# Attention in a hybrid encoder: four buffers of probabilities instead of two, and three constants of the recurrences moved into the recurrences' own pools

## The chip, the cores and the metric

The kernel runs on one core of a Trainium2 chip. The metric is the device time of one execution in microseconds (us). The core's engines work side by side, each through its own list of instructions in order: PE is TensorE's matmuls, PEld its weight loads, DVE is VectorE, ACT is ScalarE, POOL is GpSimd, SP issues most of the DMAs.

## The reference

Two layers over a sequence of 1024 tokens of width 1024. Layer 0 projects the input once and feeds two groups of heads: eight heads of windowed softmax attention with three dilations and one shared bias (A), and four heads of a gated recurrence in both directions (B). Layer 1 has twelve heads of another gated recurrence (C). Each ends in a gate, an output projection and a LayerNorm.

```
x = inputs                                          # 1 x 1024 x 1024, float32
for layer in (0, 1):
    if layer == 0:
        proj = x @ w_in_ab
        oa = dilated_attention(qa, ka, va, rel_bias)   # per pattern (1, 4, 16): s = q.k/8 + bias, |offset| <= 64 steps
                                                       # p = softmax(s); o = p.v; merged over patterns by denominators
        ob = rmsnorm(fwd_scan(q, k, v, g_f) + bwd_scan(q, k, v, g_b) - diag)
        y = (concat(oa, ob) * silu(gate)) @ w_out_ab
    else:
        y = (rmsnorm(bidirectional_scan(silu(q), 1 - f, log f, i)) * silu(gate)) @ w_out_c
    x = layer_norm(sqrt(2) * x + y) * gain + bias
```

## The kernel before, in words

All products in float32 are made of parts: each operand is split into a high part rounded to fp32r (a cast on ScalarE) and the rest (a subtraction on VectorE), and three matmuls high x high, low x high, high x low are added up in PSUM. `project` (L225 to L227) does this for the input projections: 128 output rows by 512 tokens take 8 x 3 matmuls of 512 columns. `out_units` (L247 to L249) does it for the output projections, each group of three followed by an addition to z on VectorE (L252).

The three dilated patterns of the attention are one softmax here: the bias of a key carries the logarithm of how many patterns hold it. Heads are taken in four pairs (`AttnPair`). One call of `qtile` handles 128 queries of one head: score matmuls (L571, L572) into two banks of PSUM with the tag `s`, which has two buffers; VectorE adds the bias strip in three passes and takes the running maximum (L583, 512, 64 and 128 wide), writing a tile `p` of 128 x 704; ScalarE takes the exponential and its sum; VectorE takes the reciprocal (L587) and multiplies (L588). `pv` takes two such tiles: twelve transposes on TensorE (L599) into the PSUM tiles `tr` and `kv`, high parts pH on ScalarE (L604) and low parts pL on VectorE (L605), products with the values (L608, L609, L616, L618), and a merge of the two halves of the output (L625, L626). A pair has 16 calls of `qtile` and 8 of `pv`, 32 of `pv` in all.

The low parts of the keys lie in eight tiles `kl`, whose unused half is zeroed once (`low_tile`, L461).

Constants in use: `ident` for transposes; `restart`, a row of zeros and ones that restarts the running sum of the recurrences every 16 steps (scan, L711); `mask`, for the scores of the forward direction; `ones`, which sums squares over partitions for the norm. The last three are used by layers' recurrences alone. All lie in the pool `const`, which lives through the kernel. The attention's tiles lie in a pool of their own, as do those of the GLA heads and of the HGRN heads; one is closed before the next is opened, and the tiles of the new one lie where the old one's were.

What sets the order: the program names its work as units (a projection of one block, a `qtile`, a `pv`, ...), merges the units of each head pair or head by hand-set places (`WIN`, `LAST`), and hands them to a scheduler. This gives each engine a fixed list: an instruction can be placed when its operands and a free buffer for its output are there by the scheduler's own estimate. With two buffers of `p`, the scores' passes of a third query tile are placed behind the transposes of the first. At run time each engine takes its list in order and waits for semaphores.

GpSimd's DMAs (`strip`, restored tiles `E` and `F`, gate weights `upr`) are written as descriptors into a region of SBUF whose size is `dynamic_dma_scratch_size`.

Of the kernel before, what the change touches and what calls it, by code (L numbers as in the profile page):

```python
# [7 lines left out]
F32 = mybir.dt.float32  # L8
F32R = mybir.dt.float32r
U32 = mybir.dt.uint32  # L10
# [5 lines left out]
P = 128  # L16
# [4 lines left out]
HALF = 512  # L21
# [8 lines left out]
BUCKETS, MAX_DIST = 32, 1024  # L30
# [13 lines left out]
RUN = 512  # L44
# [393 lines left out]
class AttnPair(Item):  # L438
# [92 lines left out]
    def core(self):  # L531
        T, nc, pool = self.T, self.T.nc, self.pool
        units = []
        st = {}

        def strip(j):

            t = pool.tile([P, SW], F32, tag="strip", name="strip", bufs=2)
            row = self.line[2 * self.hp + j:2 * self.hp + j + 1, :]
            st["strip", j] = t  # L540

            def src(off, step, n, w):
                return bass.AP(tensor=row.tensor, offset=row.offset + off, ap=[[1, P], [step, n], [1, w]])

            nc.gpsimd.dma_start(t[:, 0:SB].rearrange("p (b c) -> p b c", c=P), src(128, RUN, 7, P))
            nc.gpsimd.dma_start(t[:, SB:SC].rearrange("p (b c) -> p b c", c=P), src(3 * RUN, 256, 2, P))
            for h in range(2):
                tc_ = t[:, SC + 112 * h:SC + 112 * h + 112].rearrange("p (b c) -> p b c", c=16)
                for b0, n in ((0, 3), (4, 3)):
                    nc.gpsimd.dma_start(tc_[:, b0:b0 + n, :], src(b0 * RUN + 112 + 144 * h, RUN, n, 16))  # L550
                nc.gpsimd.memset(tc_[:, 3, :], -1e30)

        def qtile(j, h, r):
            if j == 0 and h == 0 and r == 0:
                self.held = {}
                self.yH = [pool.tile([P, HALF], F32R, tag="yH", name="yH", bufs=2) for _ in range(2)]
                self.yL = [pool.tile([P, HALF], F32R, tag="yL", name="yL", bufs=2) for _ in range(2)]
            if h == 0 and r == 0:
                strip(j)
            p = st[r % 2] = pool.tile([P, 704], F32, tag="p", name="p", bufs=2)  # L560
            m = pool.tile([P, 6], F32, tag="m", name="m", bufs=4)
            qi = self.q[j][h][:, r, :]
            sp = []
            for g in (h, 1 - h):
                s_ = T.ps.tile([P, HALF], F32, tag="s", name="s", bufs=2)
                if g == h:
                    out, keys = s_, lambda t: t[:, 64:KW]
                else:
                    out = s_[:, 0:2 * P].rearrange("p (b c) -> p b c", c=P)
                    keys = lambda t: bass.AP(tensor=t.tensor, offset=t.offset, ap=[t.ap[0], [64 + P * r, 2], [1, P]])  # L570
                nc.tensor.matmul(out, qi, keys(self.kh[j][g]), start=True, stop=False)  # L571
                nc.tensor.matmul(out, qi, keys(self.kl[j][g]), start=False, stop=True)  # L572
                sp.append(s_)
            t = st["strip", j]

            def rev(lo, n):
                return t[:, lo:lo + n][:, ::-1]

            parts = [(p[:, 0:512], sp[0], rev(P * r, 512)),
                     (p[:, 512:576], sp[1][:, 0:64], rev(SC + 112 * h + 16 * r, 64)),  # L580
                     (p[:, 576:704], sp[1][:, P:2 * P], rev(SB + P * h, P))]
            for n, (o, a, b) in enumerate(parts):
                nc.vector.tensor_tensor_reduce(o, a, b, 1.0, -3.0e38 if n == 0 else m[:, n - 1:n],  # L583
                                               op0=ALU.add, op1=ALU.max, accum_out=m[:, n:n + 1])
            nc.vector.tensor_scalar(m[:, 3:4], m[:, 2:3], -1.0, None, op0=ALU.mult)
            T.act(p, p, AF.Exp, bias=m[:, 3:4], accum_out=m[:, 4:5])
            nc.vector.reciprocal(m[:, 5:6], m[:, 4:5])  # L587
            nc.vector.tensor_scalar(p, p, m[:, 5:6], None, op0=ALU.mult)  # L588
# [71 lines left out]
class ScanHead(Item):  # L660
# [109 lines left out]
    def keys(self, d, hf):  # L770

        T, nc, pool, V = self.T, self.T.nc, self.pool, self.V
        r = self.pr[d, hf]
        tiles = [t for t in range(4) if hf * 4 + t != (NT - 1 if d == 0 else 0)]
        tp = T.ps.tile([P, 4, P], F32, tag="tr", name="tr", bufs=1)
        for t in tiles:
            nc.tensor.transpose(tp[:, t, :], r["k3"][:, t * P:(t + 1) * P], T.ident)  # L777
        k3T = pool.tile([P, 4, P], F32, tag="k3T", name="k3T", bufs=self.nbuf)
        lo, hi = tiles[0], tiles[-1] + 1
        nc.scalar.copy(k3T[:, lo:hi, :], tp[:, lo:hi, :])  # L780
        per = HALF // V
        order = tiles if d == 0 else tiles[::-1]
        for a in range(0, len(order), per):
            kv = T.ps.tile([P, per, V], F32, tag="kv", name="kv", bufs=1)
            for j, t in enumerate(order[a:a + per]):
                nc.tensor.matmul(kv[:, j, :], k3T[:, t, :], self.v[:, hf * 4 + t, :], start=True, stop=True)  # L786
            for j, t in enumerate(order[a:a + per]):
                i = hf * 4 + t
                nx = i + 1 if d == 0 else i - 1
                if d == 0:  # L790
                    self.stf[nx] = pool.tile([P, V], F32, tag="stf", name="stf", bufs=4)
                    dst, old = self.stf[nx], self.stf.get(i)
                else:
                    dst, old = self.stb[:, nx, :], self.stb[:, min(i, NT - 2), :]
                if i == (0 if d == 0 else NT - 1):
                    nc.vector.tensor_copy(dst, kv[:, j, :])
                else:
                    nc.vector.scalar_tensor_tensor(dst, old, r["dec"][:, t, :], kv[:, j, :],  # L798
                                                   op0=ALU.mult, op1=ALU.add)
# [296 lines left out]
def trunk_kernel(tc, x, w_in_ab, gla_gate_up, gla_gate_bias, gla_norm, w_out_ab, w_in_c, hgrn_lower_bounds,  # L1096
                 hgrn_norm, w_out_c, rel_bias, ln_gain, ln_bias, onehot, ident, mask, out):
    nc = tc.nc
    with ExitStack() as ctx:
        T = Trunk(ctx, tc)  # L1100
        c = T.const

        def load(name, shape, src, dtype=F32, eng=None):
            t = c.tile(shape, dtype, tag=name, name=name)
            (eng or nc.scalar).dma_start(t, src)
            return t

        T.ident = load("ident", [P, P], ident)
        T.mask = load("mask", [P, P], mask, U32)
        small_consts = c.tile([P, 4], F32, tag="sc", name="sc")  # L1110
        T.eps, T.epsz, T.one = (small_consts[:, i:i + 1] for i in range(3))
        for t, val in ((T.eps, EPS), (T.epsz, EPS / ALPHA ** 2), (T.one, 1.0)):
            nc.gpsimd.memset(t, val)
        T.restart = c.tile([P, HALF], mybir.dt.uint8, tag="restart", name="restart")
        nc.gpsimd.memset(T.restart, 1)
        nc.gpsimd.memset(T.restart.rearrange("p (n c) -> p n c", c=16)[:, :, 0:1], 0)
        T.ones = c.tile([P, P], F32R, tag="ones", name="ones")
        nc.scalar.copy(T.ones, T.one.broadcast_to([P, P]))
        line = T.dram.tile([A_HEADS, NLINE], F32, name="line")

        def const(name, *shape):
# [34 lines left out]
        gp, ap, hp = Phase(tc, "gla"), Phase(tc, "attn"), Phase(tc, "hgrn")  # L1156
        lr = []

        def bias_line(q):

            sl = slice(q * RUN, (q + 1) * RUN)
            oh = ap.tile([2 * BUCKETS + 2, RUN], F32, tag="p", name="oh", bufs=2)
            nc.sync.dma_start(oh, onehot[:, sl])
            ohr = ap.tile([2 * BUCKETS + 2, RUN], F32R, tag="pH", name="ohr", bufs=2)
            with tc.issue_after(T.lastact):
                nc.scalar.copy(ohr, oh)
            ps = T.ps.tile([P, HALF], F32, tag="s", name="s", bufs=2)
            with tc.issue_after(T.lastmm):
                nc.tensor.matmul(ps[0:A_HEADS], rb, ohr, start=True, stop=True)
            ls = ap.tile([A_HEADS, RUN], F32, tag="pL", name="ls", bufs=2)  # L1170
            nc.vector.tensor_copy(ls, ps[0:A_HEADS])
            nc.scalar.dma_start(line[:, sl], ls)
# [3 lines left out]
        G = [GlaHead(T, gp, h, w_in_ab[0], w_out_ab[0], gla_gate_up[0], lr, gbias, gnorm) for h in range(B_HEADS)]  # L1176
        low = {}
        A = [AttnPair(T, ap, i, w_in_ab[0], w_out_ab[0], line, low) for i in range(A_HEADS // 2)]
        H = []
# [73 lines left out]
        units = [ap.open] + tiles(start, 0, 4)  # L1253
# [3 lines left out]
        for i in range(len(A)):  # L1257
            more = G[0].spill(ap, "kh", 6, [(n, hf) for n in range(1, PARK) for hf in range(2)]) if i + 1 == len(A) else ()
            units += step(A, i, spill=more)
        units += [ap.close, gp.open] + G[0].restore() + G[0].early()  # L1260
        for i in range(len(G)):
            units += step(G, i, ln0, H[0].spill(gp, "E", 7, [(n, 0) for n in range(5)]) if i + 1 == len(G) else ())
        units += [gp.close, hp.open] + H[0].restore() + H[0].early()
        for i in range(len(H)):
            units += step(H, i, ln1)
        units += [hp.close]
# [51 lines left out]
```

## Time and profile before

| | |
|---|---|
| median of 3 runs | 2022.54 us (2022.08 to 2022.85) |
| the profiled execution | 2024.63 us, span 2022.8 us |
| PE | busy 1936.5 us, 96 % of the span, 13151 instructions |
| PEld | 1534.1 us, 76 % |
| DVE | 1302.6 us, 64 % |
| ACT | 1012.6 us, 50 % |
| POOL | 326.4 us, 16 % |
| granted clock of TensorE, mean | 0.988 |

Busy time counts the time from an instruction's start to its end, and matmuls overlap. In the views below, the share of clock is 1.00 for TensorE's upper level. "Idle before" is the time that an engine stood before an instruction, with the instruction that released it.

### The profile page before, as it was taken

How to read it: one execution, taken by the hardware profiler on the slowest of the kernel's cores; microseconds unless marked ns; L12 is line 12 of the kernel's file. 1: busy time of each engine (PE TensorE's matmuls, PEld its weight loads, DVE VectorE, ACT ScalarE, POOL GpSimd, SP SyncE). 2: the span in 40 equal slices, each digit the busy share in tenths (PEclk: the TensorE clock that was granted, in tenths of full speed). 3: DMA queues.
4: the chain of work that ended last, by engine and by line, in shares of the span. 5: the costliest groups of instructions: out<-in, count | busy, mean ns of one | idle time of the engine just before them, and what ended most of it. 6: DMA issues, size and time to landing. Idle time of an engine off the chain costs nothing.

```text
span 2022.8 us, 33771 instructions
## 1 busy us (share of the span) xinstructions
PE 1936.5 (96%) x13151; PEld 1534.1 (76%) x13151; DVE 1302.6 (64%) x2727; ACT 1012.6 (50%) x1860; POOL 326.4 (16%) x846
## 2 busy tenths in 40 slices
PE   8999999899999999988899999999999999999997
PEld 6767777777787878866678788778778877787875
DVE  4587777775676566577674746565674565666568
ACT  4555555553544444444465545445544553554463
POOL 1111010100111011012221212111211111221124
PEclk9999999999999999999999999999999999999999
DMA  5311021211211112111311111121111111111112
GB/s 144 77 33 47 20 54 27 49 53 61 63 37 48 48 38 68 47 48 44 103 53 42 48 48 32 43 63 33 38 59 41 38 43 58 32 44 53 37 53 83
DMA packets 141274, 103.73 MB, mean 51 GB/s; under 512 B 14517, under 2 KB 122933, under 8 KB 141115
## 3 DMA queue, kind: packets, MB, share of 16 engines
q1 hardware_dynamic: 129355, 89.44, 15.0%
q0 software_dynamic: 3968, 9.77, 2.1%
q10 hardware_dynamic: 7792, 2.37, 0.5%
q8 instruction: 103, 1.69, 0.3%
q14 instruction: 56, 0.46, 0.1%
HBM read 93.71 MB, written 7.85 MB: 50 GB/s over the span
## 4 chain that ended last, share of the span: by engine, by line
PE 46%; DVE 6%; ACT 5%; issue 2%; DMA 1%; POOL 1%; DVEq 0%; ACTq 0%; POOLq 0%
PE pj L225 10%; PE pj L226 10%; PE pj L227 10%; PE kv L786 3%; DVE g L711 2%; PE po L247 2%; PE po L248 2%; PE po L249 2%; PE s L812 2%; PE o L856 1%; PE o L858 1%; PE o L860 1%; DMA wraw<-in_w_out_c_dram 1%; PE tr L700 1%; PE tr L777 1%
## 5 line engine op out<-in xcount | busy, mean ns | idle before, releaser
L225 PE MATMUL pj<-xH,wH 128*128 128x512 f32 x1600 | 639.0, 399 | 1.4 <-ACT wH L187 0.9
L226 PE MATMUL pj<-xL,wH 128*128 128x512 f32 x1600 | 636.2, 398 | 0.0
L227 PE MATMUL pj<-xH,wL 128*128 128x512 f32 x1600 | 634.8, 397 | 0.0
L225 PEld LDWEIGHTS pj<-xH,wH 128*128 128x128 f32 x1600 | 302.5, 189 | 60.9 <-ACT wH L187 1.3
L227 PEld LDWEIGHTS pj<-xH,wL 128*128 128x128 f32 x1600 | 301.7, 189 | 56.4
L226 PEld LDWEIGHTS pj<-xL,wH 128*128 128x128 f32 x1600 | 302.3, 189 | 54.5
L188 DVE TENSOR_TENSOR wL<-wraw,wH 128x512 fp32r<-128x512 f32 x210 | 147.7, 703 | 183.0 <-ACT wH L187 162.0
L187 ACT CAST wH<-wraw 128x512 fp32r<-128x512 f32 x210 | 130.0, 619 | 199.4 <-PE pj L226 169.4
L731 POOL TENSOR_TENSOR eT<-gE 128x16 f32<-128x16 f32 x64 | 31.7, 495 | 1061.7 <-ACT gE L146 1061.7
L252 DVE TENSOR_TENSOR z<-z,po 128x512 f32<-128x512 f32 x200 | 136.1, 683 | 76.1 <-PE po L249 74.4
L247 PE MATMUL po<-woH,yH 128*128 128x512 f32 x336 | 138.0, 414 | 4.1 <-ACT yH L635 2.7
L248 PE MATMUL po<-woL,yH 128*128 128x512 f32 x336 | 134.2, 399 | 1.4 <-DVE woL L206 1.4
L249 PE MATMUL po<-woH,yL 128*128 128x512 f32 x336 | 131.6, 394 | 0.0
L205 ACT CAST woH<-wraw 128x512 fp32r<-128x512 f32 x80 | 47.5, 617 | 99.3 <-PE po L249 45.7
L786 PE MATMUL kv<-v,k3T 128*128 128x128 f32 (+1 forms) x448 | 80.3, 313 | 10.5 <-DVE stb L798 4.8
L247 PEld LDWEIGHTS po<-woH,yH 128*128 128x128 f32 x336 | 62.9, 189 | 32.3 <-DVE z L252 9.1
L866 ACT ACTIVATE tmp<-o 128x512 f32<-128x512 f32 x40 | 23.9, 597 | 120.9 <-PE o L858 70.8
L786 PEld LDWEIGHTS kv<-v,k3T 128*128 128x128 f32 x448 | 60.6, 190 | 30.3 <-ACT k3T L780 15.5
L678 ACT ACTIVATE F<-pj 128x512 f32<-128x512 f32 x62 | 36.7, 592 | 87.4 <-PE pj L227 87.4
L711 DVE TENSOR_TENSOR_SCAN g<-restart,g 128x512 f32<-128x512 uint8 x64 | 78.2, 1221 | 2.6 <-ACT g L146 1.8
L812 PEld LDWEIGHTS s<-q,k 128*32 128x32 f32 x2048 | 62.5, 110 | 19.5 <-issue 16.6
L248 PEld LDWEIGHTS po<-woL,yH 128*128 128x128 f32 x336 | 63.6, 189 | 14.7 <-DVE woL L206 4.9
(225 smaller groups left out, 3611.2 us busy)
## 6 DMA issues: line engine op xcount, KB each, us to landing
wraw<-in_w_in_c_dram SPq DMA_DIRECT2D x130, 256.0 KB
wraw<-in_w_in_ab_dram SPq DMA_DIRECT2D x80, 256.0 KB
wraw<-in_w_out_c_dram SPq DMA_DIRECT2D x44, 256.0 KB
wraw<-in_w_out_ab_dram SPq DMA_DIRECT2D x40, 256.0 KB
strip<-line POOLq DMA_DIRECT2D x8, 448.0 KB, 5.7
park<-sp SPq DMA_DIRECT2D x13, 256.0 KB
out_dram<-z SPq DMA_DIRECT2D x6, 512.0 KB
z<-in_x_dram SPq DMA_DIRECT2D x4, 512.0 KB
```

The costliest lines, as they stand in the source:

```text
L187: self.nc.scalar.copy(h, raw)
L188: self.nc.vector.tensor_tensor(lo, raw, h.bitcast(F32), op=ALU.subtract)
L225: mm(ps[:m], wH, xH[:, k, :], start=(k == 0), stop=False)
L226: mm(ps[:m], wH, xL[:, k, :], start=False, stop=False)
L227: self.lastmm = mm(ps[:m], wL, xH[:, k, :], start=False, stop=(k == last)).ins
L247: mm(ps, yH[:, ts], h, start=(b == 0), stop=False)
L248: mm(ps, yH[:, ts], lo, start=False, stop=False)
L249: mm(ps, yL[:, ts], h, start=False, stop=(b == nb - 1))
L252: self.nc.vector.tensor_tensor(zs, zs, ps, op=ALU.add)
L711: nc.vector.tensor_tensor_scan(run, T.restart, run, 0.0, op0=M, op1=ALU.add)
L786: nc.tensor.matmul(kv[:, j, :], k3T[:, t, :], self.v[:, hf * 4 + t, :], start=True, stop=True)
L812: mm(X[s0:s0 + 32, t, t0:t0 + n], k, q, start=True, stop=True)
```

## The change

The tag `p` gets four buffers instead of two, in `qtile` and where the one-hot tiles of the bias use the same tag. To make room in SBUF, `mask`, `restart` and `ones` leave the pool that lives through the kernel: they are made (and the mask loaded, now by a DMA of GpSimd instead of ScalarE) once when the GLA heads' pool is opened and once more when the HGRN heads' pool is opened. The region for GpSimd's descriptors shrinks from 8192 to 4096.

```diff
@@ qtile
-            p = st[r % 2] = pool.tile([P, 704], F32, tag="p", name="p", bufs=2)
+            p = st[r % 2] = pool.tile([P, 704], F32, tag="p", name="p", bufs=4)
@@ trunk_kernel
-        T.mask = load("mask", [P, P], mask, U32)
...
-        T.restart = c.tile([P, HALF], mybir.dt.uint8, tag="restart", name="restart")
-        nc.gpsimd.memset(T.restart, 1)
-        nc.gpsimd.memset(T.restart.rearrange("p (n c) -> p n c", c=16)[:, :, 0:1], 0)
-        T.ones = c.tile([P, P], F32R, tag="ones", name="ones")
-        nc.scalar.copy(T.ones, T.one.broadcast_to([P, P]))
+        def scan_consts(pool):
+            T.restart = pool.tile([P, HALF], mybir.dt.uint8, tag="restart", name="restart")
+            nc.gpsimd.memset(T.restart, 1)
+            nc.gpsimd.memset(T.restart.rearrange("p (n c) -> p n c", c=16)[:, :, 0:1], 0)
+            T.mask = pool.tile([P, P], U32, tag="mask", name="mask")
+            nc.gpsimd.dma_start(T.mask, mask)
+            T.ones = pool.tile([P, P], F32R, tag="ones", name="ones")
+            nc.scalar.copy(T.ones, T.one.broadcast_to([P, P]))
@@ bias_line
-            oh = ap.tile([2 * BUCKETS + 2, RUN], F32, tag="p", name="oh", bufs=2)
+            oh = ap.tile([2 * BUCKETS + 2, RUN], F32, tag="p", name="oh", bufs=4)
@@ the list of units
-        units += [ap.close, gp.open] + G[0].restore() + G[0].early()
+        units += [ap.close, gp.open, lambda: scan_consts(gp)] + G[0].restore() + G[0].early()
-        units += [gp.close, hp.open] + H[0].restore() + H[0].early()
+        units += [gp.close, hp.open, lambda: scan_consts(hp)] + H[0].restore() + H[0].early()
@@ kernel
-    nc = _bacc.Bacc("TRN2", target_bir_lowering=False, num_devices=1, dynamic_dma_scratch_size=8192)
+    nc = _bacc.Bacc("TRN2", target_bir_lowering=False, num_devices=1, dynamic_dma_scratch_size=4096)
```

The lists of the engines change throughout the attention. TensorE's list of before, near the end of the second head pair (the numbers tell buffers apart; `p_2289` and `p_2309` are the two tiles of one `pv`, `s_2311` and `s_2314` the second's scores, `s_2375` and `s_2378` the scores of a tile after them):

```order
L571 MATMUL s_2311<-kh_1510,q_1436 128x512
L572 MATMUL s_2311<-kl_1515,q_1436 128x512
L616 MATMUL o_2243<-pC_2275,vc_1645 128x256
L571 MATMUL s_2314<-kh_1509,q_1436 128x256
L572 MATMUL s_2314<-kl_1513,q_1436 128x256
L571 MATMUL s_2375<-kh_1512,q_1438 128x512
L618 MATMUL o_2243<-pB_2276,v_1643 128x128 x2
L572 MATMUL s_2375<-kl_1519,q_1438 128x512
L571 MATMUL s_2378<-kh_1511,q_1438 128x256
L572 MATMUL s_2378<-kl_1517,q_1438 128x256
L599 MATMUL tr_2325<-ident_87,p_2289 128x128
L599 MATMUL kv_2338<-ident_87,p_2289 128x128
```

The transposes of `p_2289` come right behind the scores. TensorE's list of the change at the same `pv` (its tiles are `p_2282` and `p_2302`; `s_2388` and `s_2391` are the scores of the fourth tile, two tiles after `p_2302`):

```order
L599 MATMUL tr_2318<-ident_87,p_2282 128x128
L599 MATMUL kv_2331<-ident_87,p_2282 128x128
L225 MATMUL pj_2579<-xH_68,wH_2460 128x512
L571 MATMUL s_2388<-kh_1505,q_1431 128x512
L572 MATMUL s_2388<-kl_1512,q_1431 128x512
L226 MATMUL pj_2579<-xL_70,wH_2460 128x512
L571 MATMUL s_2391<-kh_1504,q_1431 128x256
L572 MATMUL s_2391<-kl_1510,q_1431 128x256
L227 MATMUL pj_2579<-xH_68,wL_2461 128x512
L225 MATMUL pj_2579<-xH_68,wH_2460 128x512
L226 MATMUL pj_2579<-xL_70,wH_2460 128x512
L599 MATMUL tr_2318<-ident_87,p_2302 128x128
```

The scores of two later tiles and some projections now stand between the scores of `p_2302` and its transposes. GpSimd's list where the GLA heads' pool is opened (difference of the two lists, + is new):

```order
+L1117 MEMSET restart 128x512
+L1120 DMA mask<-in_mask_dram 128x128
+L1118 MEMSET restart 128x32
 L425 DMA E<-park 128x512 x4
 L967 MEMSET upr 32x128 x2
```

Three instructions now stand ahead of the loads of `E`; the same three stand ahead of the loads of `E` and `F` where the HGRN heads' pool is opened.

## Rows read from the trace of the kernel before

**Rows 1.** Stretches: length, busy per engine (instructions), clock, DMA share, GB/s.
```profile
core 0: us, PE busy (x) PEld busy (x) DVE busy (x) ACT busy (x) POOL busy (x), PEclk, DMA share, GB/s
91.29:481.26 389.97, 368.10 (x1935) 286.38 (x1935) 294.19 (x859) 215.55 (x463) 30.18 (x48) 0.98 0.16 40
...
193.78:276.99 83.21, 75.59 (x396) 58.36 (x396) 62.75 (x185) 45.35 (x103) 9.99 (x16) 0.96 0.17 41
```

**Rows 2.** Timeline of PE: start, length, line, operation, tiles, shapes, count.
```profile
138.52 0.39 PE L249 MATMUL po<-woH,yL 128*128 128x512 f32 x1
138.75 0.28 PE L609 MATMUL o<-pL,v 128*128 128x256 f32 x1
138.87 0.28 PE L608 MATMUL o<-pH,v 128*128 128x256 f32 x1
...
139.69 0.49 PE L599 MATMUL tr<-ident,p 128*128 128x128 f32 x3
139.94 0.47 PE L227 MATMUL pj<-xH,wL 128*128 128x512 f32 x1
```

**Rows 3.** Groups by shape on DVE, 91.29 to 481.26: busy, mean ns, idle before.
```profile
L583 DVE CUSTOM_DVE_ANT_0 p<-s,strip 128x512 f32<-128x512 f32 x60 | 41.3, 688 | 16.2 <-PE tr L599 14.3 <-PE s L572 1.6
L588 DVE TENSOR_SCALAR p<-p,m 128x704 f32<-128x704 f32 x62 | 37.2, 600 | 1.6
...
L605 DVE TENSOR_TENSOR pL<-tr,pH 128x512 fp32r<-128x512 f32 x31 | 21.4, 691 | 25.1 <-ACT pH L604 24.9
```

**Rows 4.** Timeline of PE near the end of the second head pair.
```profile
249.88 0.50 PE L571 MATMUL s<-kh,q 128*128 128x512 f32 x1 [0.69 <-DVE m L583]
...
251.40 0.39 PE L571 MATMUL s<-kh,q 128*128 128x256 f32 x1 [0.68 <-DVE m L583]
...
252.03 0.71 PE L618 MATMUL o<-pB,v 128*128 128x128 f32 x4
252.50 0.48 PE L572 MATMUL s<-kl,q 128*128 128x512 f32 x1
...
256.33 0.33 PE L599 MATMUL tr<-ident,p 128*128 128x128 f32 x1 [2.77 <-DVE p L588]
...
258.17 0.63 PE L226 MATMUL pj<-xL,wH 128*128 128x512 f32 x1
258.60 0.41 PE L608 MATMUL o<-pH,v 128*128 128x256 f32 x1
```

**Rows 5.** Waits, 91.29 to 481.26: who for whom, us in total, times, longest.
```profile
DVE pL L605 <- ACT pH L604: 24.9, 24, 1.5
...
DVE p L583 <- PE tr L599: 14.3, 20, 1.0
...
PE tr L599 <- DVE p L588: 9.2, 7, 2.8
...
PE s L571 <- DVE m L583: 7.9, 9, 1.8
```

**Rows 6.** Timeline of DVE at the place of rows 4.
```profile
249.12 0.69 DVE L583 CUSTOM_DVE_ANT_0 p<-s,strip 128x512 f32<-128x512 f32 x1 [0.41 <-PE tr L599]
...
255.58 0.70 DVE L588 TENSOR_SCALAR p<-p,m 128x704 f32<-128x704 f32 x1
...
256.50 0.59 DVE L588 TENSOR_SCALAR p<-p,m 128x704 f32<-128x704 f32 x1
```

**Rows 7.** Timeline of PE, the same place of the first and third pair.
```profile
148.89 0.90 PE L599 MATMUL tr<-ident,p 128*128 128x128 f32 x3 [2.56 <-DVE p L588]
...
363.33 0.33 PE L599 MATMUL tr<-ident,p 128*128 128x128 f32 x1 [2.77 <-DVE p L588]
```

**Rows 8.** Timeline of DVE in the first softmax passes.
```profile
75.00 0.69 DVE L206 TENSOR_TENSOR woL<-wraw,woH 128x512 fp32r<-128x512 f32 x1 [2.76 <-ACT woH L205]
```

**Rows 9.** Timeline of POOL, start and opening of the GLA heads' pool.
```profile
5.30 0.52 POOL L1115 MEMSET restart<- 128x512 uint8 x1
...
497.03 2.17 POOL L425 DMA_DIRECT2D E<-park  x4 [118.53 <-DMA park<-sp]
```

**Rows 10.** Timeline of DVE, the first scan.
```profile
515.20 1.22 DVE L711 TENSOR_TENSOR_SCAN g<-restart,g 128x512 f32<-128x512 uint8 x1
```

**Rows 11.** The strip tiles' DMAs.
```profile
DMA to landing us min/median/max: 2.6/4.8/6.6
```

## The prediction

> **What bounds the kernel now.** I read the stretches first, then the spacing of matmuls inside one, then the waits, and last one place in order of time. The part that the change reaches is the attention stage, from the merge of the first output tile to that of the last, 389.97 us [rows 1]. There TensorE is busy for 368.10 us and VectorE for 294.19 us, so TensorE looks full. It is less full than that: a matmul of 512 columns lasts about 0.39 us but the next starts 0.23 us later; 256 columns take 0.12, three transposes 0.25 [rows 2], the four pieces of L618 0.47 [rows 4]. I add these up over what the order lists between the two merges: 888 matmuls of projections and output products, 60 query tiles with 4 score matmuls each, 31 groups of 12 transposes, 9 products of 256 columns and one L618 each, and some 30 value transposes. That makes 333.8 us (estimate). TensorE therefore loses about 56 us of the 390, though its busy time shows only 21.9 us of idleness.
>
> A sentence on a rule: the Trainium skill (Perfetto Trace Analysis, Identifying the Most-Contended Engine) says that matmul busy time is a bad measure of what is left, since matmuls are pipelined; by busy time alone the change could give back 21.9 us at most, by the spacing up to 56 us, and this trace sides with the rule.
>
> To see where the 56 us go, I call a round the work between two merges (L626): two tiles of scores and softmax for one pair of queries on VectorE, and their transposes and products on TensorE. For each round I summed TensorE's need as above, and VectorE's from its mean durations: 0.69 us for the 512-wide pass, 0.60 for the normalising, 0.69 for a low part pL [rows 3], 4 % off for overlap. In 7 rounds of one head pair (193.78 to 276.99 us) both come out near 65 us (64.6 and 66.0), against 83.21 us measured [rows 1]. Taking in each round the larger of the two, all 31 rounds need 348.0 us. So 14.2 us of the loss is VectorE being the longer one in single rounds, and 42.0 us is the two waiting for each other in turn.
>
> The waits name this. TensorE waits 9.2 us for normalised probabilities (p, L588) and 7.9 us for a score bank that VectorE has not read (m, L583); VectorE waits 14.3 us before its first pass over scores for transposes, which means for one of the two buffers of p [rows 5]. The dearest place comes once in each of the first three head pairs. At 249.12 us VectorE starts a softmax as soon as transposes release a buffer, finishes the two at 255.58 and 256.50 us after other work [rows 6], and TensorE, which has no projection left between scores and transposes, stands 2.77 us at 256.33 [rows 4]. The other two are 2.56 us at 148.89 and 2.77 us at 363.33 [rows 7]. Afterwards matmuls of 512 columns start 0.43 us apart instead of 0.23 (258.17 to 258.60, rows 4): TensorE is at the lower of its two clock levels for a while.
>
> **The change part by part.**
>
> Four buffers of p. No instruction is added. The scheduler may now put the scores of two or three further tiles ahead of a group's transposes, and moves projections elsewhere. The weak place shows it: before, only the scores of one further tile stand between the last scores that a group needs and its transposes; in the change some 40 instructions do, with products and projections among them. I compared for every round the position of the first transpose (TensorE's need summed from the last merge) with that of the normalising it reads (VectorE's sum from the same merge). Before, transposes come 1.0 to 3.2 us too early in three rounds, and with no slack in two; in the change no round has less than 0.8 us of slack, and most have 1.5 to 3. So:
> - The three stops for p go: 2.56 + 2.77 + 2.77 = 8.1 us, and the slow spacing behind them. For that I take 9 matmuls at 0.20 us each time, 1.8 us and 5.4 us in all (bounds 0 and 10). Together -13.5.
> - In the same rounds TensorE first stops at the score bank (0.69 + 0.68 us, rows 4), because VectorE could not start earlier; three times, about 4.2 us. These go too, since scores are there before. -4.2.
> - The other stops for score banks (7.9 - 4.2 = 3.7 us) go by a third at most: in the change, two rounds in each of the second and third pair have scores 0.2 and 0.8 us too early for their bank. -1.2.
> - Projections move from the first seven rounds of a pair to its boundary round (59, 59 and 63 of their matmuls there before, 96, 76 and 75 in the change). In the early rounds VectorE is then the longer engine more often: the same sum of the larger need gives 351.4 us for a TensorE need of 332.8, so 18.6 us instead of 14.2. +4.4.
> - The products behind pL and pC have almost no slack (0.0 to 0.3 us) in about six rounds of the change. At half a microsecond each +3.
>
> What VectorE then waits for last is ScalarE's cast of pH and the exponentials, which the change leaves. Sum of this part: -13.5 - 4.2 - 1.2 + 4.4 + 3 = -11.5 us. The bounds are far apart: if all 42.0 us of mutual waiting went it would be -37.6 us, if none went +7.4 us. I stay near the stops that have a row.
>
> Start. The one-hot tiles use the same buffers, so four loads are issued at once and the last biases are ready about 1.2 us sooner (five projections fewer stand before them). VectorE's first softmax pass waits for the strip, but the second then sits behind a cast's low part at 75.00 us with 2.76 us of idleness [rows 8], which does not move. Between 0 and -2.7; I take -0.5. The constants' memsets and mask load that leave the start were awaited by nobody there.
>
> The constants in the two later pools. Each phase now issues on GpSimd a memset of 0.52 us, a short one, and one load, in front of the parked tiles' loads (2.17 us for four issues, 0.54 each): about 1.3 us later [rows 9]. GpSimd's queue behind them holds E's loads and the gate weights. The first scan, which needs the restart row, starts at 515.20 us [rows 10], 18 us after E's loads, so projections hide it; if the gate weights become late, 1.3 us comes through at each of two places. Between 0 and +2.6; I take +0.5 with the extra copy of the ones on ScalarE.
>
> Ring for GpSimd's descriptors, 8192 to 4096. The strips' loads land within 6.6 us of issue [rows 11], and a pair's strips are issued long before use except at the start. Between 0 and +5; I take 0.
>
> Total -11.5 us. The profiled execution took 2024.63 us around its span of 2022.8; with the change 2013.1. The median shown lies 2.1 us below that execution, so the median I forecast is 2011.0 us.
>
> **Rivals.**
>
> No gain (chance 0.17). The mutual waiting does not depend on p but keeps its size per round: each stretch grows over its sum as before (83.21 over 69.3 in seven rounds). With the new sums (59.6, 65.2 twice and 66.1, boundaries 35.1, 29.8, 30.3) that makes 391 us, +1, so 2023.5 us. For it: 24.9 us of VectorE's waiting, the largest entry, ends with ScalarE's casts of pH [rows 5], which stay. Against: the stops with the longest single waits end with p. A sentence on a rule that speaks for it: the Trainium skill (Perfetto Trace Analysis, Optimization Strategy) says that consistent bubbles can mean too little SBUF or PSUM for the next tile; were it PSUM here, this change would leave the gaps, and the trace has both releasers.
>
> Slower (0.15). Scores ahead of time block TensorE at the two score banks: TensorE takes its instructions in order, and the projections behind a blocked score wait too. Place: the J-poor early rounds of each pair, where a third tile's scores now come between the transposes and the products. A stop there cost 0.68 us [rows 4]. Paid at every third of the 120 score banks of the stage it is 27 us; the gains above are 18.9 and the costs 7.4, so the balance is 27 - 18.9 + 7.4 = +15.5, that is 2038 us. It decides from about 23 such stops on, one bank in five (15.6 us, +4).
>
> Halved ring (0.05). GpSimd stalls in issuing strips and the first strip of each pair is late by up to 6.6 us; only the start is uncovered: the gain shrinks to 4.9 us, 2017.6 us, and can be nil if later strips are late too.
>
> **How the numbers follow.** Forecast, 4 to 25 us faster: 0.58. More than 25 us: 0.05. No gain: 0.17. Slower at the banks: 0.15. Ring: 0.05. The likeliest case's own range is 1998 to 2018 us. The range that should hold 8 in 10 takes in no gain: 1998 to 2026 us. A measurement of this kernel can tell 0.2 % (4 us) from no change. Faster: 0.58 + 0.05 + 0.03 from the ring = 0.66. Within 0.2 %: most of the no-gain case and some of the ring, 0.17. Slower: 0.17.
>
> **What would show it.** Right: TensorE's stops for p (L588) in the three weak rounds gone, VectorE's waits for transposes before L583 near nil, the stage some 11 us shorter, boundary rounds longer (30 to 35 us instead of 25) but full, and no clock drop inside the stage. Wrong: score matmuls (L571) waiting for m much longer than 7.9 us in all; VectorE over 90 % busy in the early rounds; or a gain that is lost at 500 us, with the gate weights or v's transposes late. If the stage keeps 390 us although the stops for p are gone, the per-round sums are what misled me.

## The result and the profile after

The change makes the kernel faster: 1995.16 us median of 4 runs (1992.48 to 1995.26) against 2022.31 us of the kernel before beside it, ratio 0.9863, interval [0.9852, 0.9875]. That is 27.2 us, more than twice the 11.5 us forecast, and below the range. The profiled execution took 1995.26 us around a span of 1993.2 us. All runs reported below lie within 0.3 % of their kernel's median, but for one of the kernel that keeps the old order in three rounds: it took 3777.85 us for a cause not known, stands in the median of 1994.54 us (the other three have 1993.96) and is left out of the ratio.

Nearly all of it is in the attention stage, 28.5 of the 29.6 us between the two profiled spans. The first output tile is merged at 90.81 us (before 91.29), the last at 452.28 (before 481.26), and what follows lasts as long as before: 1540.9 us instead of 1541.5 (span less the last merge). Stretches of the changed kernel, the whole stage and the seven rounds of the second head pair that answer to those of [rows 1]:

```profile
core 0: us, PE busy (x) PEld busy (x) DVE busy (x) ACT busy (x) POOL busy (x), PEclk, DMA share, GB/s
90.81:452.28 361.47, 355.99 (x1927) 283.88 (x1926) 282.82 (x843) 214.21 (x459) 30.27 (x48) 1.00 0.17 42
186.50:254.29 67.79, 66.64 (x372) 52.29 (x371) 57.07 (x173) 42.88 (x98) 10.19 (x16) 1.00 0.19 41
```

The seven rounds take 67.8 us instead of 83.2 (they hold 372 matmuls instead of 396, as projections moved to the round behind them), and the granted clock is 1.00 in both where it was 0.98 and 0.96. TensorE is now idle 361.47 - 355.99 = 5.5 us in the stage, where it was 21.9. Waits of the changed kernel in the stage (engine, tile, line, waited for: us in total, times, longest):

```profile
DVE p L583 <- PE s L572: 14.3, 8, 4.1
...
PEld s L571 <- DVE m L583: 5.5, 19, 0.3
DVE pL L605 <- ACT pH L604: 5.4, 8, 1.3
PEld tr L599 <- DVE p L588: 5.3, 16, 0.5
DVE p L583 <- PE tr L599: 4.7, 7, 1.0
...
PE tr L599 <- DVE p L588: 0.2, 1, 0.2
```

Against [rows 5]: TensorE's stops for p fall from 9.2 us to 0.2, those for a score bank (PE s for m, 7.9) have no row left (the weight loads' waits, PEld, lie beside running matmuls), VectorE's wait for transposes falls from 14.3 to 4.7, and its wait for pH, which I thought the change would leave, from 24.9 to 5.4. What VectorE waits for most is now scores (14.3, in 8 waits of up to 4.1 us): it has run ahead, and that wait costs nothing as long as TensorE is busy. TensorE at the transposes that stood 2.77 us for p before (round 14, in the second pair), a timeline of its matmuls as in [rows 2]:

```profile
233.63 0.40 PE L225 MATMUL pj<-xH,wH 128*128 128x512 f32 x1
233.86 0.40 PE L226 MATMUL pj<-xL,wH 128*128 128x512 f32 x1
234.09 0.51 PE L599 MATMUL tr<-ident,p 128*128 128x128 f32 x3
234.44 0.49 PE L599 MATMUL kv<-ident,p 128*128 128x128 f32 x3
234.69 0.47 PE L227 MATMUL pj<-xH,wL 128*128 128x512 f32 x1
235.00 0.39 PE L225 MATMUL pj<-xH,wH 128*128 128x512 f32 x1
235.23 0.40 PE L226 MATMUL pj<-xL,wH 128*128 128x512 f32 x1
235.47 0.40 PE L227 MATMUL pj<-xH,wL 128*128 128x512 f32 x1
```

Transposes follow projections without a stop, and products of 512 columns start 0.23 or 0.24 us apart (0.31 once, behind the transposes); there is no 2.77 us hole and no stretch at 0.43 us behind one [rows 4, 7]. GpSimd where the GLA heads' pool opens, as in [rows 9]:

```profile
468.22 0.53 POOL L1117 MEMSET restart<- 128x512 uint8 x1 [123.19 <-DMA park<-sp]
468.89 0.58 POOL L1120 DMA_DIRECT2D mask<-in_mask_dram  x1
469.46 0.26 POOL L1118 MEMSET restart<- 128x32 uint8 x1
469.52 2.13 POOL L425 DMA_DIRECT2D E<-park  x4
```

The loads of E are issued 1.30 us after the queue could start, as worked out. It is hidden: the first scan starts at 488.30 us, 18.8 us behind E's issue (18.2 before, [rows 9, 10]).

### The profile page after: what moved, and what is told of

Same layout as the page of the kernel before. It is cut to its first block, busy times and chain, and to the rows that moved or that the text cites. A ratio compares the mean times of both kernels' runs of the same rounds, so it can differ in the third digit from the quotient of the medians.

```text
span 1993.2 us, 33807 instructions
## 1 busy us (share of the span) xinstructions
PE 1925.0 (97%) x13151; PEld 1533.8 (77%) x13151; DVE 1294.4 (65%) x2727; ACT 1014.1 (51%) x1861; POOL 327.5 (16%) x850
## 4 chain that ended last, share of the span: by engine, by line
PE 47%; DVE 6%; ACT 6%; issue 2%; POOL 1%; DMA 1%; DVEq 0%; ACTq 0%; POOLq 0%
PE pj L225 10%; PE pj L226 10%; PE pj L227 10%; PE kv L786 3%; DVE g L711 2%; PE po L247 2%; PE po L248 2%; PE po L249 2%; PE s L812 2%; PE o L856 1%; PE o L858 1%; PE o L860 1%; DMA wraw<-in_w_out_c_dram 1%; PE tr L700 1%; PE tr L777 1%
## 5 line engine op out<-in xcount | busy, mean ns | idle before, releaser
L249 PEld LDWEIGHTS po<-woH,yL 128*128 128x128 f32 x336 | 63.1, 188 | 15.3 <-DVE yL L636 1.6
```

The source lines that it names most:

```text
L249: mm(ps, yL[:, ts], h, start=False, stop=(b == nb - 1))
```

## The experiments

Times are medians; a ratio is that of a kernel to the kernel before, timed in the same call. "Stage" is from the first merge to the last in the profiled execution. "Sum" is an estimate, the working of the prediction: per round the larger of TensorE's need and VectorE's, added over 31 rounds.

| kernel | time, us | ratio, interval | stage, us | sum, us |
|---|---|---|---|---|
| before | 2022.31 | 1 | 389.97 | 348.0 |
| change | 1995.16 | 0.9863 [0.9852, 0.9875] | 361.47 | 351.4 |
| two buffers, space made | 2023.01 | 1.0006 [0.9996, 1.0015] | 390.00 | |
| three buffers | 1999.54 | 0.9886 [0.9871, 0.9901] | 364.16 | 340.4 |
| six buffers | 1992.96 | 0.9854 [0.9837, 0.9870] | 360.00 | 352.0 |
| four, old order | 2019.44 | 0.9992 [0.9983, 1.0001] | 385.55 | |
| four, old order but in 3 rounds | 2003.96 | 0.9908 [0.9891, 0.9924] | 372.44 | 348.9 |
| four, old order in 3 rounds only | 1994.54 | 0.9864 [0.9847, 0.9880] | 361.22 | 348.9 |

**Space alone.** The change with two buffers of p and of the one-hot tiles: all that makes room stays, and the gain must go.

```diff
-p = st[r % 2] = pool.tile([P, 704], F32, tag="p", name="p", bufs=4)
+p = st[r % 2] = pool.tile([P, 704], F32, tag="p", name="p", bufs=2)
```

> The changed kernel with two buffers of p again (and two for the one-hot tiles): what is left of the change is the move of mask, restart and ones into the pools and the halved descriptor region. TensorE's list in the attention stage is then word for word that of the kernel before. Theory (the whole gain is waiting between TensorE and VectorE that goes because the scheduler's lists put slack between scores and transposes): 2022 us, within 2 us of before. Rival (the constants, the start or the ring carry part of it): 2017 us or less. If the loads added on GpSimd cost something that the 27 us hide: 2024 to 2026 us.

2023.01 us, ratio 1.0006 [0.9996, 1.0015]. The constants in the later pools, the mask's load on GpSimd and the halved region for descriptors cost nothing that can be told from noise (at most 3 us, by the interval); the rival of the halved ring falls. The whole gain hangs on the buffers. The stage is the same to 0.03 us as before (merges at 92.09 and 482.09 us), and in a second profile of the change it is 361.52 us, so its length repeats far better than the whole time.

**How many buffers.** Three (bufs=3 in both lines), and six (room for them from low key tiles taken in turn from four instead of eight, `% 4` to `% 2` where `self.kl` is set).

> The changed kernel with three buffers of p. Per round of the attention stage the larger of TensorE's and VectorE's need sums to 340.4 us (four buffers: 351.4, two: 348.0), no transposes come too early in the lists (least slack over 0.5 us, median 1.2 us; four: 1.5, two: 1.0 with three rounds below -1). Theory (stage = this sum + about 10 us of rest as in the changed kernel): stage 350 to 355 us, 1984 to 1989 us, that is faster than four buffers. Rival (each further tile in flight gives more; three is half the way): 2005 to 2012 us.

> The changed kernel with six buffers of p, for which four of the eight low key tiles are given up (each key tile is then reused by the next head pair instead of the one after). Sum of the larger need 352.0 us, slack median 1.5 us, as with four buffers. Theory: within 3 us of the changed kernel, 1992 to 1998 us. Rival (each further tile in flight gives more): below 1988 us.

Three buffers give 1999.54 us, 0.9886 [0.9871, 0.9901], 83 % of the gain (0.0114 of 0.0137); six give 1992.96 us, 0.9854 [0.9837, 0.9870], not told apart from four by the intervals, as the theory there had it. For three buffers both expected ranges were missed. Three buffers have the lowest sum of all, 340.4 us, and yet a stage 2.7 us longer than four (364.16): the sum alone doesn't order the kernels. What it leaves out, the waiting beyond it, is 42.0 us before, 23.8 with three buffers, 10.1 with four, 8.0 with six.

**Buffers without the new order.** Four buffers, but the first softmax pass of a tile (L583) is issued behind the low part pL of the output product before it, as the two buffers had forced it.

```diff
+                with ExitStack() as es:
+                    if n == 0 and T.lastpl is not None:
+                        es.enter_context(T.tc.issue_after(T.lastpl))
...
+                    lastpl = nc.vector.tensor_tensor(pL, tp, pH.bitcast(F32), op=ALU.subtract).ins
+                    if kg == 1:
+                        T.lastpl = lastpl
```

> The changed kernel with four buffers of p, but on VectorE's list the first pass over the scores of each tile is kept behind the low part pL of the key tiles of the last transposed group (an order of the list alone, no wait), as two buffers made it. The lists then have transposes too early by 1.6 to 3.3 us in three rounds again, as before. Theory (the gain is in the lists' order): 2020 to 2026 us, as before. Rival (the gain is the free buffer at run time, VectorE no longer waiting for transposes, whatever the lists say): 2005 us or less.

2019.44 us, 0.9992 [0.9983, 1.0001]: almost nothing of the gain is left, 0.08 % of 1.37 % (4.4 us of the stage's 28.5), and the rival's 2005 us is refuted. The four buffers are there, and no first pass waits for one (the 14.3 us of before, DVE p for tr, have no row); what is missing is the order of the lists. TensorE's timeline of this kernel (L602 is L599 here) has the three stops back, where before had 2.56, 2.77 and 2.77 us [rows 4, 7]:

```profile
147.61 0.90 PE L602 MATMUL tr<-ident,p 128*128 128x128 f32 x3 [2.83 <-DVE p L591]
...
252.76 0.33 PE L602 MATMUL tr<-ident,p 128*128 128x128 f32 x1 [2.64 <-DVE p L591]
...
357.70 0.47 PE L602 MATMUL tr<-ident,p 128*128 128x128 f32 x1 [2.64 <-DVE p L591]
```

Waits of the same kernel in its stage, 90.93 to 476.48:

```profile
DVE pL L608 <- ACT pH L607: 21.6, 23, 1.5
PEld tr L602 <- DVE p L591: 19.1, 31, 3.1
...
PE tr L602 <- DVE p L591: 9.3, 7, 2.8
...
PE s L571 <- DVE m L586: 2.9, 8, 0.9
```

TensorE's stops at score banks shrink from 7.9 to 2.9 us, its stops for p stay (9.3, before 9.2), and the weight loads of the transposes (PEld tr) wait 19.1 us for p, where the same view of before has 15.8:

```profile
PEld tr L599 <- DVE p L588: 15.8, 25, 3.0
```

**The three places and the rest.** The same edit with a count of the output products, once everywhere but in the three weak rounds, once only in them:

```diff
-                    if n == 0 and T.lastpl is not None:
+                    if n == 0 and T.lastpl is not None and T.npair not in (6, 14, 22):
```

> The complement: four buffers, the old order in every round but 6, 14 and 22. The sum of the larger need is 348.9 us; the median slack of the transposes falls from 1.54 to 1.27 us, six rounds have -0.2 to 0.4 us. Theory (spread waiting): most of what the old order everywhere cost (24.3 us) is lost here, stage 375 to 383 us, time 2009 to 2017 us. Rival (the three places carry the gain): 17.7 us of the 24.3 stay won, time 2002 us or less.

> Four buffers, and the old order (a softmax's first VectorE pass behind the low part pL of the output product before it) only in rounds 6, 14 and 22, where TensorE stood for p longest in the kernel before; all other rounds as in the changed kernel. The sum of the larger need is 348.9 us (351.4 in the change), the slack of the transposes there falls to -0.2 to 0.3 us. Theory (the gain was waiting spread over all rounds, the three places are a small part of it): the stage is 361 to 368 us, the time 1995 to 2003 us. Rival (the forecast's sizing: the three places carry 8.1 us of stops for p, 5.4 us of slow spacing and 4.2 us of stops at the score bank, 17.7 us): 2013 us.

Old order elsewhere: 2003.96 us, 0.9908 [0.9891, 0.9924]. Both theories missed: 2009 to 2017 was one, 2002 or less the other. Old order in the three rounds only: 1994.54 us, 0.9864 [0.9847, 0.9880], no loss at all, just below the theory's range; the rival's 2013 us is refuted. Stretches of the three kernels' stages, in the order old everywhere, old elsewhere, old in three rounds only:

```profile
90.93:476.48 385.55, 367.19 (x1933) 287.32 (x1933) 293.23 (x853) 215.69 (x461) 31.35 (x48) 0.98 0.16 40
```

```profile
89.81:462.25 372.44, 361.41 (x1933) 284.46 (x1933) 292.07 (x852) 215.27 (x461) 29.88 (x48) 1.00 0.16 41
```

```profile
88.30:449.52 361.22, 357.15 (x1927) 283.37 (x1926) 283.78 (x842) 213.70 (x459) 30.39 (x48) 1.00 0.17 42
```

So the 28.5 us come in steps of 4.4 (before to old everywhere), 13.1 (the three rounds freed, and the clock goes from 0.98 to 1.00) and 11.0 us (the order freed elsewhere). The steps don't add in every order: with the other rounds free, the three may keep the old order at no cost, since the rounds before them arrive with slack: by the lists the transposes of the three then come 0.2 us too early to 0.3 us late enough, with the old order everywhere 1.6 to 3.3 us too early. With the other rounds old, two stops are left, one round behind the freed ones (L603 is L599 here):

```profile
256.30 0.55 PE L603 MATMUL tr<-ident,p 128*128 128x128 f32 x3 [1.26 <-DVE p L592]
...
357.43 0.55 PE L603 MATMUL tr<-ident,p 128*128 128x128 f32 x3 [1.11 <-DVE p L592]
```

Where the steps lie shows in the starts of TensorE's matmuls. For each matmul, take the time to the next start, less the usual spacing of its form [rows 2, 4], and add this up by rounds, numbered 1 to 31 from merge to merge. What is left is TensorE's lost time, in us:

| rounds | before | four, old order | old order but in 3 | change |
|---|---|---|---|---|
| 5, 6, 13, 14, 21, 22: the weak rounds and those before | 24.9 | 26.4 | 10.6 | 6.8 |
| 7, 15, 23: those behind | 3.8 | 4.3 | 8.6 | 3.7 |
| 10, 11, 18, 19 | 12.8 | 6.0 | 5.7 | 4.6 |
| the other 18 | 20.4 | 21.3 | 20.1 | 19.3 |
| all | 61.9 | 58.0 | 44.9 | 34.4 |

So the waiting was not spread over all rounds, as the theory had it. Of the 27.5 us won, 18.1 are in the first row and 8.2 in the third; the other 18 rounds lose about 1.1 us each in every kernel, and the last pair (rounds 25 to 31) loses 6.0 us with two buffers and 5.9 with four. In the same way 10.0 of the 10.5 us between the old order elsewhere and the change lie beside the freed rounds, in 5, 13, 21 and 7, 15, 23. The third row is a second place, in the second and third pair, most of which goes with four buffers even in the old order; by what is not shown. (Old order in the three rounds only loses 34.1 us in all.) TensorE in round 10 of the kernel before:

```profile
214.27 0.39 PE L609 MATMUL o<-pL,v 128*128 128x256 f32 x1 [0.34 <-DVE pL L605]
...
216.49 0.50 PE L571 MATMUL s<-kh,q 128*128 128x512 f32 x1 [0.68 <-DVE m L583]
...
217.85 0.71 PE L618 MATMUL o<-pB,v 128*128 128x128 f32 x4 [0.52 <-ACT pB L615]
...
219.80 0.50 PE L571 MATMUL s<-kh,q 128*128 128x512 f32 x1 [0.99 <-DVE m L583]
```

The granted clock in the 10 us from 222 to 232, behind these stops, is 0.91. How much of a row is stops and how much the slower clock behind them is not told apart. In VectorE's list of the change, four first passes, not two, stand ahead of the first group's pL in each of the first three pairs; this lead of two tiles is kept to the last rounds of the pair, where the dearest stops were.

**What is left.** If the stage were the sum plus some 10 us, VectorE's excess over TensorE (351.4 - 332.8 = 18.6 us) would be what can still be won. In these kernels ScalarE does the normalising (L588), for all tiles, for every second, for all but the first four, and the last with six buffers.

```diff
-            nc.vector.tensor_scalar(p, p, m[:, 5:6], None, op0=ALU.mult)
+            nc.scalar.activation(p, p, AF.Copy, scale=m[:, 5:6])
```

> As the change, but the normalising of p (L588, 62 times 0.60 us on VectorE) is done by ScalarE. Output unchanged. Sums over rounds: VectorE 306.1 to 270.0 us, ScalarE 220 to some 263 us, TensorE 330; the largest of the three per round 342.8 us instead of 351.4. Theory (the stage is the sum of the longest need per round and about 10 us of remaining waiting, so VectorE's excess of 18.6 us is what is left to gain): stage 351 to 354 us, time 1985 to 1988 us. Rival (ScalarE's casts of pH and its exponentials come later behind the added work, and VectorE's waits for them grow by what its need shrinks): time 1993 to 2005 us.

> As the run before it, but only every second tile's normalising goes to ScalarE (31 instead of 62). Sum of the longest need per round 345.5 us. Theory: stage 354 to 358 us, time 1987 to 1991 us. Rival (ScalarE's queue becomes the chain): 1993 to 2000 us, less late than with all of them moved.

All tiles: 1994.15 us, 0.9863 [0.9849, 0.9878]. Every second: 1996.93 us, 0.9878 [0.9863, 0.9892], and a stage of 359.97 us. Neither is told apart from the change, and both times lie where the rival had them. With all, the stage is 354.97 us, 1 us above my theory's range (351 to 354), but its first merge comes at 95.41 us instead of 90.81. ScalarE's timeline there:

```profile
80.30 0.87 ACT L588 ACTIVATE p<-p,m 128x704 f32<-128x704 f32 x1
81.19 1.28 ACT L526 ACT_TABLE_LOAD   x1
82.48 0.60 ACT L526 ACTIVATE sg<-pj 128x512 f32<-128x512 f32 x1
83.09 1.28 ACT L141 ACT_TABLE_LOAD   x1
84.39 0.62 ACT L187 CAST wH<-wraw 128x512 fp32r<-128x512 f32 x1
84.91 0.88 ACT L588 ACTIVATE p<-p,m 128x704 f32<-128x704 f32 x1
```

The second tile's normalising stands behind two function table loads, an activation and a cast; in the change, on VectorE, the first two were done at 80.43 us (79.84 + 0.59). The first four tiles went back:

> As the run with all normalising on ScalarE, but the first four query tiles, whose ScalarE work stood behind two function table loads before the first merge, keep it on VectorE. Output unchanged. Theory (what that run won in the stage, 6.5 us, it lost before the first merge, 4.6 us): first merge back at 91 us; the sum of the longest need per round is 340.4 us by TensorE and VectorE (347.6 with ScalarE), with 10 to 12 us of waiting the stage is 351 to 359 us and the time 1985 to 1993 us. Rival (the start only moves the loss: what stands ahead of the first merge is paid back behind it): stage about 360 us, 1994 us or more.

> The run beside it with six buffers of p and the low key tiles taken in turn from four instead of eight, as in the six-buffer run (2.2 us better than the change). Sum of the longest need 346.2 us by TensorE and VectorE, 350.1 with ScalarE. Theory: more projections go to the boundary rounds, so it wins less than the run beside it or nothing: stage 356 to 361 us, time 1990 to 1995 us. Rival (deeper buffers add their 2.2 us whatever bounds the rounds): 2 us below the run beside it.

1993.66 us, 0.9864 [0.9849, 0.9879], and with six buffers 1991.59 us, 0.9854 [0.9837, 0.9870]. The first merge is back at 90.02 us, and the stage has grown again, by 3.8 us: most of what is won at the start is given back in the stage, as the rival had it. The time, 1993.66, lies between the two ranges (up to 1993, from 1994). Six buffers are 2.1 us below, as the rival there had it, with intervals that overlap. Stages of the run with all tiles, all but four, and all but four with six buffers:

```profile
95.41:450.38 354.97, 350.15 (x1908) 282.20 (x1907) 253.89 (x773) 257.35 (x516) 29.11 (x48) 1.00 0.17 43
```

```profile
90.02:448.80 358.78, 353.64 (x1927) 285.68 (x1926) 255.94 (x782) 258.73 (x519) 29.20 (x48) 1.00 0.17 43
```

```profile
90.21:447.73 357.52, 354.19 (x1928) 285.53 (x1927) 255.13 (x782) 257.14 (x519) 29.37 (x48) 1.00 0.17 43
```

VectorE is 27 to 29 us less busy than in the change, and the last merge comes 1.9 to 4.6 us earlier. TensorE is idle 4.8, 5.1 and 3.3 us, and its lost time by the starts is 31.3, 31.5 and 30.2 us (change 34.4), so it is TensorE that is nearly full. My theory that VectorE's excess is paid falls, and with it the reading of the 10.1 us as waiting. As ScalarE has 43 to 45 us more to do in these kernels, what room on VectorE alone is worth is not shown. About 20 of the 30 us lost are in the 18 rounds without a weak place, alike in every kernel; whether they can be won is open.

The best version and the change again, on one chip:

> The changed kernel itself, timed beside the version below on the same chip, since the two have not shared one yet: 1992 to 1996 us.

> The version with six buffers and all but four tiles normalised on ScalarE again. Theory (TensorE is the bound of the stage in both, with 5.5 and 3.3 us of idle time left in it, so only what lies below 4 us can come): 2 to 4 us below the changed kernel. Rival (its lead was the chip of that call): no difference, within 1 us.

The change 1995.71 us, 0.9873 [0.9854, 0.9892]; the version with six buffers and ScalarE's normalising 1992.72 us, 0.9860 [0.9838, 0.9882]. It lay 3.6 us (against the change's first timing) and 3.0 us lower, as expected, but the intervals overlap: probably better than the change, surely than before.

## Why the prediction was wrong

The direction and the mechanism held: the stops for p in the three weak rounds went, the boundary rounds grew and are full (36.4, 29.7 and 30.3 us instead of 25.1, 25.1 and 26.3), no clock drop is left inside the stage, the start and the pool openings cost what was said or nothing. The size of the terms beside the three places failed. By the table of lost time:

- Three places, -13.5 and -4.2, together -17.7: rounds 5, 6, 13, 14, 21 and 22 lose 18.1 us less. About right together, but the part for score banks doesn't exist by itself: with four buffers and the old order the stops at the banks shrink, and these rounds lose 26.4 us instead of 24.9. What is taken away at the scores comes back at the transposes there.
- The first failed step is "The other stops for score banks (7.9 - 4.2 = 3.7 us) go by a third at most", -1.2. Rounds 10, 11, 18 and 19, where these stops stand, lose 8.2 us less. The four long bank stops there are 3.3 us (0.68 and 0.99 in each pair); the stops for products between them and the slower clock behind were not counted.
- The second failed step is the cost, "+4.4" for VectorE as the longer engine and "+3" for products behind pL and pC. It is not seen: the other 21 rounds lose 1.2 us less instead of 7.4 more. VectorE ran ahead and TensorE was nearly full. These two steps make 7.0 and 8.6 of the 16.0 us between the forecast's -11.5 and the -27.5 in the table.
- "What VectorE then waits for last is ScalarE's cast of pH ... which the change leaves" is wrong: 24.9 us became 5.4. That VectorE had waited for the cast because its list gave it no other tile's pass to do fits the run with four buffers and the old order, where the wait is still 21.6 us.
- The working has slips that move no term by more than 1 us: with the spacings as printed, TensorE's need is 327.8 us, not 333.8, so it loses 62 us and not 56; 255.58 and 256.50 us are where the last passes of the two softmaxes start, not where they end. The 391 us of the first rival can't be redone from the one ratio that it gives.

The rivals: no gain and slower at the banks are refuted by the time and the waits (PEld s for m 5.5 us, no wait above 0.3), the halved ring by the run with space alone.

On the rule that matmul busy time is a bad measure of what is left (the Trainium skill, Perfetto Trace Analysis, Identifying the Most-Contended Engine): this case agrees; busy time left 21.9 us to win, and 28.5 came. On the rule that consistent bubbles can mean too little SBUF or PSUM (the Trainium skill, Perfetto Trace Analysis, Optimization Strategy): it was SBUF here, but almost only through the order; with the buffers and the old order the ratio is 0.9992.

## What to carry to other kernels

When two engines work in turn on a pair of buffers, price a deeper pool round by round: add up what the busier engine's starts lie beyond their usual spacing, and ask of every round that loses more than the rest what goes there, with the slower clock behind it. The rounds of the dearest stops gave two thirds of the gain here, a second place most of the rest, and the rounds without a stop next to nothing. Test a deeper pool by holding the order fixed, since the gain may be the scheduler's: here it was lost although the buffers were there. A wait removed at one of two places in a cycle (scores, transposes) can come back at the other.

## What the runs showed of the hardware

Normalising 128x704 takes 884 ns on ScalarE (60 of them, 52.9 us) and 586 ns on VectorE. Groups of the run with all tiles on ScalarE, and of the change:

```profile
L588 ACT ACTIVATE p<-p,m 128x704 f32<-128x704 f32 x60 | 52.9, 884 | 5.3 <-DVE m L587 5.1
```

```profile
L588 DVE TENSOR_SCALAR p<-p,m 128x704 f32<-128x704 f32 x60 | 35.2, 586 | 1.0
```

Moving it makes room on VectorE and costs half as much again on ScalarE, and the stage got 2.7 to 6.5 us shorter by it (358.78 and 354.97 us instead of 361.47), the whole time by nothing clear of noise. The granted clock of the stage follows the stops: freeing the three rounds of the old order, with the same number of matmuls, took it from 0.98 to 1.00.
